# A hybrid decoder block on one core: block sums begun earlier in the attention, nine modulation rows moved into the values' and gates' products

## Chip, core and metric

The kernel runs on one core of one Trainium2 chip. The metric is the device time of one execution in microseconds; the median of several executions is given. All data are f32. Activations are kept transposed: features on the 128 partitions, the 512 tokens along the free axis.

The engines are named as in the profile: PE is TensorE (PEld its weight loads), DVE is VectorE, ACT is ScalarE, POOL is GpSimd, SP is SyncE, which issues most of the DMAs. Each engine works through its own queue in the order in which the program gave it the instructions.

## The reference, cut to what matters

```python
mod = silu(c) @ w_ada + b_ada                  # 9 vectors of 1024: shift, scale, gate of three sub-layers
u = rmsnorm(h) * (1 + sc1) + sh1
h = h + 0.5 * gt1 * swiglu(u)                  # first feed-forward
u = rmsnorm(h) * (1 + sc2) + sh2
h = h + gt2 * token_mixing(u)                  # <- the change is here
u = rmsnorm(h) * (1 + sc3) + sh3
h = h + 0.5 * gt3 * swiglu(u)                  # second feed-forward
return rmsnorm(h)

def token_mixing(u):                           # u: 512 x 1024
    p, q, k, v, gate_logits = split(u @ w_in)  # 256, 768, 768, 768, 2048 columns
    y_pool = multiscale_pool(p)                # trailing means over 2, 4, 8, 16 tokens
    q, k = rope(q), rope(k)                    # 12 heads of 64
    # three groups of four heads, dilations 1, 4, 16, causal windows;
    # the groups are merged by their softmax denominators
    y_attn = merged_dilated_attention(q, k, v)
    g_pool, g_attn = split(sigmoid(gate_logits))
    return (g_pool * (y_pool @ w_pb) + g_attn * (y_attn @ w_ab)) @ w_out
```

## The kernel before

**Matmuls in three parts.** Each f32 operand is split into a high part (ACT copies it into a rounded format: `whi`, `UH`) and a low part (DVE subtracts: `wlo`, `UL`), and each product is three matmuls: high x high, high x low, low x high. So each weight tile costs one DMA, one copy of 128 x 1024 on ACT (line 378) and one subtraction of the same size on DVE (line 390).

**Products in 2 x 2 blocks.** Wide products (values, gates, feed-forward) are computed in seven half-size block products in place of eight, in the manner of Strassen. These need sums of blocks of the weights (DVE, line 313, and DMAs that accumulate, issued by POOL, line 321) and sums of blocks of u. For the token mixer `mix_sums` makes the sums of u: `whole(i)` adds high and low part of a quarter of u (line 1323), `x0`, `x1`, `x2`, `x3` subtract such quarters from each other (lines 1334 and 1335), `hi(i)` and `lo(i)` split the results (ACT line 1327, DVE line 1331), and `last` writes the fourth one back into `UH` and `UL`. All are of 128 x 1024. The sums stand in buffers `x0`, `x1`, `x2` and `q0`; the split parts go to `uc`, `s0`, `k0`, `x2`, `v1`, `x0`.

**Modulation rows.** The 72 rows of `w_ada` (128 outputs each) are worked off in the background: `bg` makes DVE multiply one row of 128 x 1024 by silu(c) and add it up (line 449, in `ada_do`), then `bg_fetch` queues the DMA of a next row on SP (line 441) into a buffer of the list `ada_free`, as far ahead as `ada_depth` allows. A DMA into a buffer that is still being read waits, and SP's queue behind it waits too. `ada_stop` bounds how far the rows go.

**Order in `mix`.** The order is written out by hand. After the head (queries and keys of group 0) and the values of group 0 come two pool tiles, then eight tiles of queries and keys of groups 1 and 2 (`mm_tile`, 24 matmuls of 128 x 512 each), and then

- `value_duo`: the values of groups 1 and 2, in seven block products P0 to P6 of 24 matmuls of 128 x 256, on three PSUM banks A, B, C. The list of products is A (P0), B, A, C, A, B, A: each time that A is used again, a copy on ACT (line 1816) has carried away what it held. Bank C, into which A is copied after P0, is the bank of the last query and key tile.
- `gate_duo`, four times: seven block products each for the gates; the first in `mix`, the others in `merge_out`, which also does the branches and the output product.

`hooks` places other work at positions 0 to 7 inside a query and key tile (before the matmuls of that eighth): a list of pairs (position, function). At position 5 stand the attention's steps for group 0: values of the step before last, transposes (line 1486), scores (line 1453), exponentials (`at_exp`: reductions and maxima on DVE, lines 1469 and 1471, exponentials on ACT, line 1474). The rotary embedding of a tile is `rope_a` after it (ACT line 1394, DMAs on SP that exchange partitions, DVE multiply with the tile's bank, line 1398) and `rope_b` in the next tile at position 6 (DVE lines 1416 and 1420). The steps for groups 1 and 2 lie in the middle of P2, P4 and P6 of `value_duo` and of P1, P3 and P5 of the first `gate_duo` (the argument `within`); the argument `beside` holds what is done after a product.

Weights are fetched into three buffers and split three to four tiles ahead (`look`). The fetch of a tile is queued on SP when the program has given out the last use of a buffer.

The positions of the sums in the kernel before:

```python
sums = {4: [(7, lambda: u["whole"](0))],
        5: [(1, lambda: u["whole"](2)), (4, u["x0"]), (6, lambda: u["hi"](0)), (7, lambda: u["whole"](1))],
        6: [(1, u["x2"]), (3, u["x1"]), (5, lambda: u["lo"](0)), (7, lambda: u["whole"](3))],
        7: [(0, lambda: u["hi"](1)), (0, lambda: u["hi"](2)), (1, u["x3"]), (3, lambda: u["lo"](2)),
            (5, lambda: u["lo"](1))]}
```

Tiles 0 to 3 hold a modulation row each at position 7, tile 1 another at position 2: rows 51 to 55. Row 56 follows in the first gate block, rows 57 to 59 in the block after it.

Of the kernel before, what the change touches and what calls it, by code (L numbers as in the profile page):

```python
# [8 lines left out]
F32 = mybir.dt.float32  # L9
# [5 lines left out]
P = 128  # L15
T = 512
HT = 256
D = 1024
# [147 lines left out]
class Kernel:  # L166
# [5 lines left out]

    def plan(self):
        (i1, o1), mix, (i2, o2) = chunk_widths()
        self.chunks = []
        for name, ws in (("wf1i", i1), ("wf1o", o1), ("wmix", mix), ("wf2i", i2), ("wf2o", o2)):
# [267 lines left out]
    def ada_do(self, j, n=1):  # L444
        t, mod = self.adat.pop(j), self.mod[:, j:j + 1]
        for i in range(n):
            c = slice(i * D // n, (i + 1) * D // n)
            o = self.part if i else mod
            self.nc.vector.scalar_tensor_tensor(t[:, c], t[:, c], 1.0, self.cond[:, c], op0=OP.mult, op1=OP.mult,
                                                accum_out=o)  # L450
            if i:
                self.nc.vector.tensor_tensor(mod, mod, o, op=OP.add)
        if self.ada_free is not None:
            self.ada_free.append(t)

    def ada_fin(self, which, j0, j1, g=None):
# [273 lines left out]
    def step(self):  # L730

        self.now += 1
        due = [f for t, f in self.put if t <= self.now]
        self.put = [x for x in self.put if x[0] > self.now]
        for f in due:
            f()
# [874 lines left out]
    def mix(self):  # L1611
# [6 lines left out]
        mp = outer.enter_context(tc.tile_pool(name="mx", bufs=1))  # L1618

        x = [mp.tile([P, D], F32, name=f"x{i}") for i in range(3)]  # L1620
# [4 lines left out]
        with tc.tile_pool(name="rt", bufs=1) as self.rt, tc.tile_pool(name="aw", bufs=2) as self.aw:  # L1625
# [19 lines left out]
            self.bg_fetch()  # L1645
            self.head(1, bk, AF.Exp, [self.bg] * 5)
            assert self.ada_next == 45 and not self.adat, self.ada_next
            self.ada_free, self.ada_stop, self.ada_depth = list(x), 56, 2
            self.bg_fetch()

            to = [(self.qt[0], 0), (self.qt[0], 1), (self.kt[0], 0), (self.kt[0], 1)]
# [14 lines left out]
            for n in range(4):  # L1666
# [3 lines left out]
                b = self.nb()  # L1670
# [22 lines left out]
            def hooks(new, extra=(), between=()):  # L1693
                sc, old = pipe
                todo = [(self.at_values, old), (self.at_turn, sc), (lambda f: f(), between), (self.at_scores, new),
                        (self.at_exp, new)]
                h = {5: [lambda f=f, u=u: f(u) for f, us in todo for u in us]}
                for k, f in extra:
                    h.setdefault(k, []).append(f)
                pipe[0], pipe[1] = list(new), sc  # L1700
                return h


            todo = [x for n in range(4) for x in ([(0, n, hp) for hp in range(2)], [])]
            self.p1 = mp.tile([P, D], F32, name="s0")[:, :528]
            for t in range(2):
                self.pool_diff(t, self.mm_tile(hooks(todo.pop(0), [(7, self.bg)])))
            todo += [[], []]
            rest = []
            u = self.mix_sums([*x, self.qt[0]], [[wide(mp, "uc"), wide(mp, "s0")], [wide(ma, "k0"), wide(mp, "x2")],  # L1710
                                                 [wide(ma, "v1"), wide(mp, "x0")]])
            sums = {4: [(7, lambda: u["whole"](0))],
                    5: [(1, lambda: u["whole"](2)), (4, u["x0"]), (6, lambda: u["hi"](0)), (7, lambda: u["whole"](1))],
                    6: [(1, u["x2"]), (3, u["x1"]), (5, lambda: u["lo"](0)), (7, lambda: u["whole"](3))],
                    7: [(0, lambda: u["hi"](1)), (0, lambda: u["hi"](2)), (1, u["x3"]), (3, lambda: u["lo"](2)),
                        (5, lambda: u["lo"](1))]}
            for n, (dst, hp) in enumerate((y[g], hp) for g in (1, 2) for y in (self.qt, self.kt) for hp in range(2)):
                more = [(2, self.bg)] if n == 1 else []
                if n == 6:
                    self.X, self.retired = [self.AR, self.cs, self.v23.rearrange("p c f -> p (c f)")[:, D:]], []  # L1720
                    self.ready = True
                b = self.mm_tile(hooks(todo.pop(0), rest + more + sums.get(n, [(7, self.bg)])))
                rt = [self.scratch(2 * i + hp)[:, :T] for i in range(2)]
                self.rope_a(b, dst, hp, *rt)

                rest = [(6, lambda dst=dst, hp=hp, w=rt[1]: self.rope_b(dst, hp, w))]


            assert self.ada_next == 56 and not self.adat, self.ada_next

            def clear():
                v.memset(self.fT.bitcast(F32), 0.0)
# [3 lines left out]
            g23 = [[(1, c, hp) for hp in range(2)] for c in range(4)]  # L1736
            step = lambda c=None: [lambda: [f() for f in hooks(g23[c] if c is not None else [])[5]]]
            p5 = self.ev[:, 2 * T:3 * T]
            self.value_duo(p5, {0: rest[0][1], 1: u["last"]}, {2: step(0), 4: step(1), 6: step(2)})

            def rows():
                self.ada_free, self.ada_stop, self.ada_depth = [self.qt[2]], 60, 1
                self.bg_fetch()

            def third():
# [3 lines left out]
                self.pool_map(two(ma, "k2"), two(mp, "x1"))  # L1749

            used = self.gate_duo(self.qt[1], self.kt[1], p5, lambda n=1: None,
                                 {2: lambda: (self.at_swap(), rows()), 3: clear, 4: self.at_merge, 5: self.bg, 6: third}, {},
                                 {1: step(3), 3: step(), 5: step()})
            at = [t[:, i * T:(i + 1) * T] for i in range(2) for t in (self.qt[1], self.kt[1])]
            spread = [self.bS[1], self.bO] + self.bT
# [6 lines left out]
        def second():  # L1762
            self.at_high(0)
            self.at_y(spread, 1)

        self.merge_out(at, {0: lambda: (self.at_fT(spread[0]), self.bg()), 1: ends, 2: second, 3: lambda: (self.at_high(1), self.at_low(0)),
                            4: lambda: self.at_low(1), 5: self.bg, 6: self.bg}, ma, mp)
        outer.close()

# [189 lines left out]
    def build(self):  # L1959
        nc, tc, ctx, a = self.nc, self.tc, self.ctx, self.a  # L1960
        ctx.enter_context(tc.manual_schedule())
        per = ctx.enter_context(tc.tile_pool(name="per", bufs=1))
        psum = ctx.enter_context(tc.tile_pool(name="psum", bufs=1, space=bass.MemoryType.PSUM))
        self.plan()
        tl = lambda n, w, dt=F32: per.tile([P, w], dt, name=n)
        self.free = [tl(f"raw{i}", CW) for i in range(3)]

        self.hi, self.lo = tl("whi", RING, F32R), tl("wlo", RING, F32R)
        self.vecs = tl("vecs", 106)
        self.Hall = tl("H", KT * T)  # L1970
        self.H = [self.Hall[:, k * T:(k + 1) * T] for k in range(KT)]
        tl("pad0", 16)
        self.UHv = tl("UH", KT * T, F32R)
        cst, self.eps = tl("cst", 163), tl("eps", 1)
        tl("pad1", 16)
        self.ULv = tl("UL", KT * T, F32R)
        self.UH, self.UL = ([x[:, k * T:(k + 1) * T] for k in range(KT)] for x in (self.UHv, self.ULv))
        self.AR = tl("AR", 2 * T)
        self.acc, self.R = self.AR[:, :T], self.AR[:, T:]
        self.mod, self.part = tl("mod", 72), tl("part", 1)  # L1980
        self.hpi, self.r4 = tl("hpi", 1), tl("r4", 4)
        early = ExitStack()
        ep = early.enter_context(tc.tile_pool(name="early", bufs=1))
        el = lambda n, w, dt=F32: ep.tile([P, w], dt, name=n)
        self.cond = el("cond", D)
        self.ones = tl("ones", P)
        self.invf, self.sign, self.icnt, self.ident = cst[:, 0:1], cst[:, 1:2], cst[:, 3:35], cst[:, 35:163]
        self.cst = cst
        self.cs = el("cs", 2 * T)
        self.cos, self.sin = self.cs[:, :T], self.cs[:, T:]  # L1990
        tl("pad", 32)
        self.ev, self.turn = tl("ev", 4 * T), 0
        self.tr = el("tr", 5 * P)
        self.pi = self.tr[:, 4 * P:].bitcast(I32)
        self.B = [psum.tile([P, T], F32, name=f"bank{i}") for i in range(8)]
        self.banks, self.bi = self.B[:6], 0
        self.adat = {}
        self.todo = []
        dram = ctx.enter_context(tc.tile_pool(name="dram", bufs=1, space=bass.MemoryType.DRAM))
        self.scr = dram.tile([T, 8], F32, name="scr")  # L2000
        self.scr2 = dram.tile([32, 2 * T], F32, name="scr2")

        self.ada_free, self.ada_depth = None, 3
        with self.open_ffn():
            self.ada_pool = ExitStack()
            self.adaw = self.ada_pool.enter_context(tc.tile_pool(name="f1a", bufs=4))
            self.put, self.now = [], 0
            self.startup()
            self.ffn(0, FIRST)
            self.sums.close()  # L2010
        self.mix()
        early.close()
        with self.open_ffn(True) as self.f2:
            self.sums, self.retired = self.open_sums(), []
            self.ffn2()
# [185 lines left out]
```

## Time and profile before

| | |
|---|---|
| median of 3 runs | 978.46 us (976.54 to 983.93) |
| profiled execution | 980.78 us, span of its instructions 977.9 us |
| mean granted clock of PE | 0.993 |
| PE busy | 960.6 us (98%) |
| DVE busy | 850.9 us (87%) |
| ACT busy | 549.4 us (56%) |
| POOL busy | 90.8 us (9%) |
| moved by DMA | 173.67 MB |

Times in the views are microseconds from the first instruction of the span. In a timeline each row has the start, the duration, the engine, the line, the operation, what it writes and reads, and in brackets how long the engine was idle before it and what ended this. In the windows each row has the stretch, its length, the busy time of PE, PEld, DVE, ACT and POOL with the number of instructions, the clock that PE was granted as a share of full speed, the share of the DMA engines that was busy, and GB/s.

### The profile page before, as it was taken

How to read it: one execution, taken by the hardware profiler on the slowest of the kernel's cores; microseconds unless marked ns; L12 is line 12 of the kernel's file. 1: busy time of each engine (PE TensorE's matmuls, PEld its weight loads, DVE VectorE, ACT ScalarE, POOL GpSimd, SP SyncE). 2: the span in 40 equal slices, each digit the busy share in tenths (PEclk: the TensorE clock that was granted, in tenths of full speed). 3: DMA queues.
4: the chain of work that ended last, by engine and by line, in shares of the span. 5: the costliest groups of instructions: out<-in, count | busy, mean ns of one | idle time of the engine just before them, and what ended most of it. 6: DMA issues, size and time to landing. Idle time of an engine off the chain costs nothing.

```text
span 977.9 us, 18361 instructions
## 1 busy us (share of the span) xinstructions
PE 960.6 (98%) x7366; PEld 905.3 (93%) x7366; DVE 850.9 (87%) x1255; ACT 549.4 (56%) x837; POOL 90.8 (9%) x107
## 2 busy tenths in 40 slices
PE   9999999999999999998999999999999999999997
PEld 7888999999999899777898998898999999999997
DVE  7989999899998788899668887989899888989885
ACT  5443666565745553554675553465666657566655
POOL 0000100110100003810000000000101010110002
PEclk9999999999999999998999999999999999999999
DMA  9856785776868458634447655722766766665632
GB/s 350 280 181 249 208 235 148 208 198 152 235 178 251 138 170 272 215 103 115 112 132 222 166 130 174 252 93 89 194 150 195 173 151 164 171 172 142 169 80 87
DMA packets 54088, 173.67 MB, mean 178 GB/s; under 512 B 7793, under 2 KB 10481, under 8 KB 54002
## 3 DMA queue, kind: packets, MB, share of 16 engines
q1 hardware_dynamic: 44272, 140.24, 43.3%
q0 software_dynamic: 9152, 31.72, 18.0%
q8 instruction: 57, 0.93, 0.4%
q10 hardware_dynamic: 578, 0.53, 0.2%
q14 instruction: 29, 0.24, 0.1%
HBM read 135.36 MB, written 2.24 MB: 141 GB/s over the span
## 4 chain that ended last, share of the span: by engine, by line
PE 84%; DVE 9%; issue 2%; ACT 2%; DMA 2%; POOL 0%; SPq 0%; POOLq 0%; DVEq 0%; ACTq 0%
PE bank L752 12%; PE bank L753 12%; PE bank L754 12%; PE bank L422 8%; PE bank L423 8%; PE bank L424 8%; PE bank L1112 4%; PE bank L1113 4%; PE bank L1111 4%; DVE wlo L390 2%; PE bank L2123 2%; PE bank L2127 1%; PE bank L2125 1%; DMA cs<-wada 1%; ACT prob L1474 1%
## 5 line engine op out<-in xcount | busy, mean ns | idle before, releaser
L390 DVE TENSOR_TENSOR wlo<-raw,whi 128x1024 fp32r<-128x1024 f32 (+3 forms) x155 | 167.5, 1092 | 36.5 <-ACT whi L378 36.3
L752 PE MATMUL bank<-UH,whi 128*128 128x256 f32 x672 | 186.1, 277 | 0.0
L753 PE MATMUL bank<-UL,whi 128*128 128x256 f32 x672 | 185.7, 276 | 0.0
L754 PE MATMUL bank<-UH,wlo 128*128 128x256 f32 x672 | 185.7, 276 | 0.0
L390 DVE TENSOR_TENSOR wlo<-X,whi 128x1024 fp32r<-128x1024 f32 (+3 forms) x138 | 142.7, 1047 | 16.9 <-ACT whi L378 16.7
L378 ACT ACTIVATE whi<-raw 128x1024 fp32r<-128x1024 f32 (+3 forms) x155 | 142.9, 939 | 20.7 <-DMA raw<-wf1o 8.7
L378 ACT ACTIVATE whi<-X 128x1024 fp32r<-128x1024 f32 (+3 forms) x138 | 123.5, 918 | 51.1 <-DVE X L313 46.8
L752 PEld LDWEIGHTS bank<-UH,whi 128*128 128x128 f32 x672 | 126.3, 188 | 2.1 <-issue 1.9
L753 PEld LDWEIGHTS bank<-UL,whi 128*128 128x128 f32 x672 | 126.2, 188 | 0.0
L754 PEld LDWEIGHTS bank<-UH,wlo 128*128 128x128 f32 x672 | 126.2, 188 | 0.0
L754 PE MATMUL bank<-SH,wlo 128*128 128x256 f32 x408 | 112.7, 276 | 0.2 <-DVE wlo L390 0.2
L752 PE MATMUL bank<-SH,whi 128*128 128x256 f32 x408 | 112.7, 276 | 0.0
L753 PE MATMUL bank<-SL,whi 128*128 128x256 f32 x408 | 112.6, 276 | 0.0
L422 PE MATMUL bank<-UH,whi 128*128 128x512 f32 (+1 forms) x272 | 92.7, 341 | 0.0
L423 PE MATMUL bank<-UL,whi 128*128 128x512 f32 (+1 forms) x272 | 91.8, 337 | 0.1
L424 PE MATMUL bank<-UH,wlo 128*128 128x512 f32 (+1 forms) x272 | 91.5, 336 | 0.0
L754 PEld LDWEIGHTS bank<-SH,wlo 128*128 128x128 f32 x408 | 76.6, 188 | 0.4 <-DVE wlo L390 0.4
L752 PEld LDWEIGHTS bank<-SH,whi 128*128 128x128 f32 x408 | 76.6, 188 | 0.0
L753 PEld LDWEIGHTS bank<-SL,whi 128*128 128x128 f32 x408 | 76.6, 188 | 0.0
L1111 PE MATMUL bank<-HI,whi 128*128 128x256 f32 x224 | 61.8, 276 | 0.0
L1112 PE MATMUL bank<-HK,whi 128*128 128x256 f32 x224 | 61.8, 276 | 0.0
L1113 PE MATMUL bank<-HI,wlo 128*128 128x256 f32 x224 | 61.8, 276 | 0.0
(430 smaller groups left out, 2462.7 us busy)
## 6 DMA issues: line engine op xcount, KB each, us to landing
raw<-wmix SPq DMA_DIRECT2D x44, 512.0 KB, 4.4
raw<-wf1i SPq DMA_DIRECT2D x32, 512.0 KB, 5.7
raw<-wf2i SPq DMA_DIRECT2D x30, 512.0 KB, 3.7
ada<-wada SPq DMA_DIRECT2D x23, 512.0 KB, 5.6
X<-raw POOLq DMA_DIRECT2D x23, 512.0 KB, 5.3
x<-wada SPq DMA_DIRECT2D x22, 512.0 KB, 5.0
X<-wf2i SPq DMA_DIRECT2D x14, 512.0 KB, 4.6
X<-wf1i SPq DMA_DIRECT2D x11, 512.0 KB, 4.6
```

The lines of the kernel that those rows point to most:

```text
L378: self.nc.scalar.activation(self.hi[:, y], r[:, x], AF.Copy)
L390: self.nc.vector.tensor_tensor(self.lo[:, y], r[:, x], self.hi[:, y], op=OP.subtract)
L422: M(ps, hi, uh, start=start, stop=False)
L423: M(ps, hi, ul, start=False, stop=False)
L424: M(ps, lo, uh, start=False, stop=stop)
L752: M(o, hi, uh, start=start and p == 0 and k == 0, stop=False, skip_group_check=True)
L753: M(o, hi, ul, start=False, stop=False, skip_group_check=True)
L754: M(o, lo, uh, start=False, stop=k == 3, skip_group_check=True)
L1111: M(o, hi, uh, start=start and m % 2 == 0 and k == 0, stop=False, skip_group_check=True)
L1112: M(o, hi, ul, start=False, stop=False, skip_group_check=True)
L1113: M(o, lo, uh, start=False, stop=k == 1, skip_group_check=True)
L2123: M(b, hi, self.UH[k], start=k == 0, stop=False)
```

## The change

The sums of u start at tile 1 in place of tile 4, and are spread over tiles 1 to 7. The modulation rows stop at 51 in place of 56 before the value block: the five in tiles 0 to 3 are taken out. Rows 51 to 59 are then placed after P1, P3 and P5 of `value_duo`, after products 0, 2, 5 and 6 of the first gate block and, as before, after products 5 and 6 of the next one. They use the buffer `x1`, loaded one row at a time, and from row 57 on `q2`; `x1` is not given back after its last row (`ada_gone`), since `pool_map` needs its place.

```diff
-        if self.ada_free is not None:
+        if self.ada_free is not None and t is not self.ada_gone:
             self.ada_free.append(t)
...
-            self.ada_free, self.ada_stop, self.ada_depth = list(x), 56, 2
+            self.ada_free, self.ada_stop, self.ada_depth = list(x), 51, 2
...
-            sums = {4: [(7, lambda: u["whole"](0))],
-                    5: [(1, lambda: u["whole"](2)), (4, u["x0"]), (6, lambda: u["hi"](0)), (7, lambda: u["whole"](1))],
-                    6: [(1, u["x2"]), (3, u["x1"]), (5, lambda: u["lo"](0)), (7, lambda: u["whole"](3))],
-                    7: [(0, lambda: u["hi"](1)), (0, lambda: u["hi"](2)), (1, u["x3"]), (3, lambda: u["lo"](2)),
-                        (5, lambda: u["lo"](1))]}
+            sums = {1: [(1, lambda: u["whole"](0))], 2: [(1, lambda: u["whole"](2)), (5, u["x0"])],
+                    3: [(0, lambda: u["hi"](0)), (1, lambda: u["whole"](1))], 4: [(1, u["x2"]), (4, u["x1"])],
+                    5: [(1, lambda: u["whole"](3)), (3, lambda: u["hi"](1)), (4, u["x3"]), (6, lambda: u["lo"](0))],
+                    6: [], 7: [(0, lambda: u["hi"](2)), (1, lambda: u["lo"](2)), (4, lambda: u["lo"](1))]}
...
-                more = [(2, self.bg)] if n == 1 else []
...
-                b = self.mm_tile(hooks(todo.pop(0), rest + more + sums.get(n, [(7, self.bg)])))
+                b = self.mm_tile(hooks(todo.pop(0), rest + sums.get(n, [])))
...
-            assert self.ada_next == 56 and not self.adat, self.ada_next
+            assert self.ada_next == 51 and not self.adat, self.ada_next
+            row = mp.tile([P, D], F32, name="x1")
+            self.ada_free, self.ada_stop, self.ada_depth = [row], 60, 1
+            self.bg_fetch()
...
-            self.value_duo(p5, {0: rest[0][1], 1: u["last"]}, {2: step(0), 4: step(1), 6: step(2)})
+            self.value_duo(p5, {0: rest[0][1], 1: lambda: (u["last"](), self.bg()), 3: self.bg, 5: self.bg}, {2: step(0), 4: step(1), 6: step(2)})
...
             def rows():
-                self.ada_free, self.ada_stop, self.ada_depth = [self.qt[2]], 60, 1
+                self.ada_free.append(self.qt[2])
+                self.ada_gone = row
                 self.bg_fetch()
...
-                                 {2: lambda: (self.at_swap(), rows()), 3: clear, 4: self.at_merge, 5: self.bg, 6: third}, {},
+                                 {0: self.bg, 2: lambda: (self.at_swap(), self.bg(), rows()), 3: clear, 4: self.at_merge, 5: self.bg, 6: lambda: (third(), self.bg())}, {},
...
-        self.merge_out(at, {0: lambda: (self.at_fT(spread[0]), self.bg()), 1: ends, 2: second, 3: lambda: (self.at_high(1), self.at_low(0)),
+        self.merge_out(at, {0: lambda: self.at_fT(spread[0]), 1: ends, 2: second, 3: lambda: (self.at_high(1), self.at_low(0)),
```

More of the change, by code (lines that the diff above doesn't have):

```diff
@@ L2001, in build @@
         self.scr2 = dram.tile([32, 2 * T], F32, name="scr2")
-        self.ada_free, self.ada_depth = None, 3
+        self.ada_free, self.ada_depth, self.ada_gone = None, 3, None
         with self.open_ffn():
```

## The prediction

> **What bounds the kernel now.** I read the page first, then the waits of TensorE (PE), then the stretch of the change in 2 us windows, then the timelines of PE, VectorE (DVE) and ScalarE (ACT) there.
>
> ```profile
> span 977.9 us, 18361 instructions
> ...
> PE 960.6 (98%) x7366; PEld 905.3 (93%) x7366; DVE 850.9 (87%) x1255; ACT 549.4 (56%) x837; POOL 90.8 (9%) x107
> ```
>
> PE is busy 98% of the span, and the change leaves its matmuls as they are. So all that can be won is PE idle time and time at a lowered clock. The view of PE's waits between 380 and 620 us, which holds the whole token mixer, has two rows (total, times, longest):
>
> ```profile
> PE bank L1834 <- ACT bank L1816: 4.3, 1, 4.3
> PE bank L1834 <- ACT v L1816: 2.3, 1, 2.3
> ```
>
> Both are in `value_duo`. The windows show what follows each wait (columns: PE, weight loads, DVE, ACT, POOL busy, granted clock, DMA share, GB/s):
>
> ```profile
> 456.00:458.00 2.00, 0.00 (x0) 0.00 (x0) 1.97 (x3) 0.00 (x0) 0.00 (x0) 1.00 1.03 197
> 458.00:460.00 2.00, 0.25 (x1) 0.25 (x2) 2.00 (x3) 0.88 (x2) 0.00 (x0) 0.66 0.01 0
> 460.00:462.00 2.00, 2.00 (x10) 2.00 (x11) 1.46 (x3) 2.00 (x4) 0.00 (x0) 0.50 0.00 0
> 462.00:464.00 2.00, 2.00 (x16) 1.78 (x16) 1.97 (x3) 1.04 (x2) 0.00 (x0) 0.50 0.53 127
> 464.00:466.00 2.00, 2.00 (x16) 1.78 (x13) 2.00 (x5) 0.00 (x0) 0.00 (x0) 0.63 0.62 193
> ...
> 478.00:480.00 2.00, 0.58 (x2) 0.58 (x3) 0.00 (x0) 2.00 (x6) 0.00 (x0) 0.78 0.36 102
> 480.00:482.00 2.00, 2.00 (x11) 2.00 (x10) 1.66 (x2) 1.26 (x2) 0.00 (x0) 0.50 0.00 0
> 482.00:484.00 2.00, 2.00 (x23) 1.60 (x23) 2.00 (x4) 0.00 (x0) 0.87 (x1) 0.86 0.36 70
> ```
>
> After the wait that ends at 459.75, PE runs at clock 0.50 until about 465.5 (the 0.63 window is half-rate for three quarters): 5.7 us at half rate, 2.9 us lost. After the one that ends at 479.42 it is half-rate until about 482.55 (0.86): 3.1 us, 1.6 lost. **At stake: 4.3 + 2.9 + 2.3 + 1.6 = 11.1 us.**
>
> Next, why PE waits. I call the value block's products P0 to P6, and tiles 0 to 7 the query and key tiles of groups 1 and 2.
>
> ```profile
> 449.61 0.28 PE L1834 MATMUL bank<-whi,UH 128*128 128x256 f32 x1
> 452.43 0.38 PE L1834 MATMUL bank<-whi,uc 128*128 128x256 f32 x1
> 459.75 0.58 PE L1834 MATMUL bank<-whi,k 128*128 128x256 f32 x1 [4.32 <-ACT bank L1816]
> 470.58 1.04 PE L1486 MATMUL bank<-cst,prob 128*128 128x128 f32 x8
> 471.56 1.16 PE L1453 MATMUL bank<-k,q 64*128 64x128 f32 x16
> 479.42 0.58 PE L1834 MATMUL bank<-whi,UH 128*128 128x256 f32 x1 [2.26 <-ACT v L1816]
> ```
>
> ```profile
> 459.12 0.58 ACT L1816 ACTIVATE bank<-bank 128x512 f32<-128x512 f32 x1 [5.83 <-DVE k L1398]
> ...
> 468.43 0.58 ACT L1816 ACTIVATE v<-bank 128x512 f32<-128x512 f32 x1
> ...
> 478.79 0.57 ACT L1816 ACTIVATE v<-bank 128x512 f32<-128x512 f32 x1
> ```
>
> P0 starts at 449.61, P1 at 452.43: 2.8 us a product. P2 (459.75) waits until ACT has copied bank A into bank C at 459.12, and ACT waited 5.83 us for DVE, whose rope multiply (L1398) of tile 7 still had to read bank C, 9 us after PE had filled it. P6 (479.42) waits for the copy of 478.79, which stands in ACT's queue behind the exponentials of an attention step, and these behind DVE's reductions. Both are a late DVE:
>
> ```profile
> 402.48 1.22 DVE L449 SCALAR_TENSOR_TENSOR x<-x,cond 128x1024 f32<-128x1024 f32 x1
> ...
> 404.47 0.69 DVE L1398 TENSOR_TENSOR q<-bank,cs 128x512 f32<-128x512 f32 x1 [0.77 <-ACT tr L1394]
> ...
> 407.48 2.08 DVE L449 SCALAR_TENSOR_TENSOR x<-x,cond 128x1024 f32<-128x1024 f32 x1
> ...
> 412.64 1.61 DVE L449 SCALAR_TENSOR_TENSOR x<-x,cond 128x1024 f32<-128x1024 f32 x1
> ...
> 421.03 1.22 DVE L449 SCALAR_TENSOR_TENSOR x<-x,cond 128x1024 f32<-128x1024 f32 x1
> ...
> 425.51 0.69 DVE L1416 TENSOR_TENSOR rt<-rt,cs 128x512 f32<-128x512 f32 x1 [1.52 <-DMA rt<-tr]
> ...
> 426.84 1.22 DVE L449 SCALAR_TENSOR_TENSOR x<-x,cond 128x1024 f32<-128x1024 f32 x1
> ...
> 433.45 1.22 DVE L1323 TENSOR_TENSOR x<-UH,UL 128x1024 f32<-128x1024 f32 x1
> ...
> 458.34 0.68 DVE L1398 TENSOR_TENSOR k<-bank,cs 128x512 f32<-128x512 f32 x1
> ...
> 461.84 0.68 DVE L1416 TENSOR_TENSOR rt<-rt,cs 128x512 f32<-128x512 f32 x1
> ...
> 465.44 0.41 DVE L1469 CUSTOM_DVE_ANT_0 prob<-bank,masks 128x256 f32<-128x256 f32 x1
> ...
> 469.99 1.23 DVE L390 TENSOR_TENSOR wlo<-v,whi 128x1024 fp32r<-128x1024 f32 x1 [2.70 <-ACT whi L378]
> ...
> 475.75 0.42 DVE L1469 CUSTOM_DVE_ANT_0 prob<-bank,masks 128x256 f32<-128x256 f32 x1
> ```
>
> ```profile
> 450.00:460.00 10.00, 5.68 (x48) 5.45 (x47) 9.93 (x12) 2.49 (x4) 0.89 (x1) 0.93 0.51 124
> 460.00:470.00 10.00, 10.00 (x71) 9.55 (x72) 6.66 (x17) 6.59 (x15) 0.00 (x0) 0.73 0.49 159
> ...
> 490.00:500.00 10.00, 10.00 (x100) 9.39 (x99) 4.48 (x13) 7.28 (x16) 0.00 (x0) 1.00 0.37 109
> ```
>
> DVE works 9.93 of the 10 us before 460. From 426 to 460 it has one queue without a hole. So here DVE is the bound: PE follows it at three points, tile 7's multiply (458.34), the first attention step's reductions (465.44), the second's (475.75).
>
> **The change, part by part.** *Five modulation rows (51 to 55) leave tiles 0 to 3.* They are the five L449 rows above. A 1.22 us operation holds the queue 1.14 us (426.84 to the accumulator read at 427.99). The one at 402.48 is worth nothing: the multiply at 404.47 then waits for ACT anyway. The others give 2.0 + 1.5 + 1.1 + 1.1, and 0.2 for the bias addition after the last: 6.0 us.
>
> *Four of the sums (whole 0, whole 2, x0, whole 1) move from tiles 4 to 6 into tiles 1 to 3.* Their number is the same. But two run while GpSimd still computes the pools; there the row at 407.48 took 2.08 where its like takes 1.22. Whether a sum does too isn't shown; between 1.14 and 2.0 each I take 2.0 and 1.9, since a row of the same size in the same place took that: 1.6 us lost, at least 0. The 1.5 us hole ahead of 425.51 is filled by the sums: 1.5 won. A new hole of some 1.0 us opens in tile 5: x2 and x1 now stand ahead of tile 4's reductions, so ACT gets to its next weight copy 1 us later. Sum: -6.0 + 1.6 - 1.5 + 1.0 = **-4.9, so tile 7's multiply starts at 453.4 (bounds 452 to 455)**. ACT's copy then ends at 454.1; P2 wants it at 449.6 + 2 x 2.8 = 455.2. The first wait goes, and its half clock with it.
>
> *What is late next.* Between the multiply (458.34) and the first step's reductions (465.44) DVE needs 7.1 us: two weight remainders, the rope sum at 461.84, a third remainder, the last sum. Row 51 now stands there as well: 1.1. So the reductions start at 453.4 + 7.1 + 1.1 = 461.6. From them to the end of ACT's copy, 468.43 + 0.58 - 465.44 = 3.6 us: 465.2. P4 needs this copy. PE reaches P4 at 455.2 + two products (5.6) + 1.1 for the step's scores + 0.5, since the last scores read the rope sum, done at 453.4 + 3.5 + 1.3 = 458.2 where they could have ended at 457.7: 462.4. **A new wait of about 2.8 us ahead of P4.** In the old run this copy ended at 469.0.
>
> *P6.* From the first reductions to the second, 475.75 - 465.44 = 10.3 us, of them 2.70 idle for ACT (469.99), which stays. Row 52 adds 1.1: 461.6 + 11.4 = 473.0. Copy done 3.6 later: **P6 starts at 476.6 in place of 479.42, 2.8 us earlier.** PE is free for it at 465.2 + 4.9 (P4 with 2.1 of transposes and scores) + 2.8 = 472.9, or 1.7 later if the clock halves after P4's wait; either is before 476.6, so that halving costs nothing, and a second wait of 2 to 3.7 us is left.
>
> *Loads.* A row's load is queued on SP behind the release of the single buffer `x1`, so it stops the weight loads behind it until DVE has done the row before.
>
> ```profile
> raw<-wmix SPq DMA_DIRECT2D x10, 512.0 KB, 5.0
> ```
>
> Row 52's load waits for row 51 (done 461.5), ahead of the second load of the gate block, which would have been free about 459. Landed 5.0 us later, that is 467, just when DVE gets to the sum that reads it. Cost taken 0.3, bounds 0 to 3.
>
> *Rows 53 to 59.* They lie in the gate block and the first block after it, where DVE is busy 4.48 of 10 us and PE waits nowhere. I take 0; the cover is DVE's idle time. The row after 56 goes into another buffer (`q2`), so SP doesn't wait there. One row less in the merge: 0.
>
> *Clock after P6.* The old wait of 2.26 us cost 1.6; one of 2 to 3.7 us costs between 0 and 2.9. I take the same 1.6.
>
> **Sum: -2.8 + 0.3 = -2.5 us** on the profiled execution of 980.78 (span 977.9, 2.9 around it), so 978.3. The median of the runs is 978.46, 2.3 lower; from there **976.0 us**.
>
> **Rivals.** (a) *Both waits go.* If DVE reaches the first step 3 us earlier than I think (the sums at 1.14 under GpSimd, no new hole: 2.6 us), P4 doesn't wait, and the second wait shrinks too: down to -11.1, 967.4; half of it, 971. For it: every wait is the same late DVE. Against: two of the five rows come back ahead of the last wait. (b) *No halving after P6*, as a short wait split over two stretches of the clock's watch might pass: -4.1, 974.4. For it: the new wait needn't lie as the old one did. Against: clock 0.50 after 2.26 us. [...] (c) *Nothing moves*: ACT and not DVE sets P4 and P6; DVE idled 2.70 us for it before 469.99. Then 978 to 979. (d) *Slower: the row on SP starves the gate weights.* Place: row 52 ahead of the second gate load. Price: DVE waits for that load in front of the second step's reductions, one us of PE for each us. It decides from 2.8 us on, so if three loads of 512 KB queued at once take over 8 us where one takes 5.0; at 10 us, P6 at 481.5 with its half clock, +2 to +3: 981. Against it: DMA share 0.5 there. (e) *The change doesn't do what it says*, a row's load or a buffer's release holding the sums back to their old places: as (c).
>
> **How the numbers follow.** Forecast (-1 to -4 us) 0.55; (a) 0.17, of it 0.07 by nearly all; (b) 0.08; (c) and (e) 0.12; (d) 0.08. Leaving out the end of (a) and half of (d): 968.5 to 981. The runs of before spread from 976.54 to 983.93, so about 1% (9.8 us) is what a measurement can tell from no change: faster 0.07 (the end of (a)), slower 0.02 (from (d)), within 0.91.
>
> **What would show it.** Right: no PE wait for the copy from bank A to bank C; tile 7's multiply about 4 us after PE's last matmul in its bank, not 9; a wait of 2 to 3 us on L1834 ahead of P4 for a copy into v23, and one ahead of P6; the clock at 0.5 in one or two windows; no wait in the gates. Wrong: DVE with holes before tile 7 (then its relief was smaller), no wait at P4 (rival a), DVE waiting for a DMA ahead of a weight sum (rival d), or a new PE wait after 500 us.

## The result, and the profile after

The changed kernel takes 976.81 us in the median of 20 runs (974.04 to 978.88), the kernel before 979.38 (976.54 to 983.93). The ratio is 0.9973, 95% interval 0.9962 to 0.9984: **2.6 us less, 0.3%**. The profiled execution has a span of 975.8 us where before had 977.9. Lines of the changed kernel lie two further down from `value_duo` on (L1834 is L1836, L1816 is L1818), and those of the experiments up to six.

The head of the page, with instructions as before and nearly the same busy times:

```profile
span 975.8 us, 18361 instructions
...
PE 957.7 (98%) x7366; PEld 902.1 (92%) x7366; DVE 849.4 (87%) x1255; ACT 548.7 (56%) x837; POOL 90.7 (9%) x107
```

PE's waits between 380 and 620 us (total, times, longest):

```profile
PE bank L1836 <- ACT v L1818: 5.6, 2, 3.5
PE bank L1544 <- DVE x L1609: 0.8, 1, 0.8
PE bank L1504 <- DVE v L1850: 0.8, 1, 0.8
PE bank L1486 <- ACT prob L1474: 0.3, 1, 0.3
```

Before there were two, of 4.3 and 2.3 us. The one for the copy from bank A into bank C is gone. Two for copies into `v23` are there, together 5.6 us, and three short ones that are new. PE's timeline says where (start, duration, operation, idle time before it):

```profile
449.93 0.28 PE L1836 MATMUL bank<-whi,UH 128*128 128x256 f32 x1
...
452.76 0.28 PE L1836 MATMUL bank<-whi,uc 128*128 128x256 f32 x1
...
455.58 0.28 PE L1836 MATMUL bank<-whi,k 128*128 128x256 f32 x1
...
464.79 0.39 PE L1836 MATMUL bank<-whi,v 128*128 128x256 f32 x1 [2.10 <-ACT v L1818]
...
476.30 0.39 PE L1836 MATMUL bank<-whi,UH 128*128 128x256 f32 x1 [3.45 <-ACT v L1818]
```

P0, P1 and P2 follow each other 2.83 us apart, without a hole. P4 waits 2.10 us and P6 3.45. So 6.6 us of waiting became 7.5 in other places. The waiting itself didn't shrink; in this profile the gain is the half clock that followed both waits of before (4.5 us by the prediction's reckoning) and follows neither of these. The windows behind the two waits:

```profile
464.00:466.00 2.00, 1.21 (x10) 1.21 (x11) 0.28 (x1) 2.00 (x5) 0.00 (x0) 1.00 0.94 365
...
478.00:480.00 2.00, 1.21 (x17) 0.80 (x18) 2.00 (x4) 0.14 (x1) 0.87 (x1) 1.00 0.00 0
```

The granted clock is 1.00 throughout, where the same stretch of before has 0.50. This isn't how most runs went: 16 of the 20 were granted 0.996 or 0.997 in the mean, against 0.999 here. Yet those 16 average 976.5 us and the two at 0.999 976.3, so the difference hardly shows in the time. A stretch of 3.41 us at half clock takes 0.0017 off the mean (1.7 of 975.8 us), so in most runs there is room for one such stretch; where it lay there isn't known.

DVE's timeline, with the rows that answer to those of before (L390 makes the low part of a weight tile, the weight remainder):

```profile
406.28 1.23 DVE L390 TENSOR_TENSOR wlo<-raw,whi 128x1024 fp32r<-128x1024 f32 x1 [0.27 <-ACT whi L378]
407.42 2.08 DVE L1323 TENSOR_TENSOR x<-UH,UL 128x1024 f32<-128x1024 f32 x1
...
413.20 1.21 DVE L390 TENSOR_TENSOR wlo<-raw,whi 128x1024 fp32r<-128x1024 f32 x1
414.33 1.24 DVE L1323 TENSOR_TENSOR x<-UH,UL 128x1024 f32<-128x1024 f32 x1
...
451.73 0.68 DVE L1398 TENSOR_TENSOR k<-bank,cs 128x512 f32<-128x512 f32 x1
452.78 1.23 DVE L390 TENSOR_TENSOR wlo<-raw,whi 128x1024 fp32r<-128x1024 f32 x1 [0.37 <-ACT whi L378]
454.53 1.23 DVE L390 TENSOR_TENSOR wlo<-raw,whi 128x1024 fp32r<-128x1024 f32 x1 [0.53 <-ACT whi L378]
456.29 0.69 DVE L1416 TENSOR_TENSOR rt<-rt,cs 128x512 f32<-128x512 f32 x1 [0.53 <-DMA rt<-rt]
...
461.17 0.42 DVE L1469 CUSTOM_DVE_ANT_0 prob<-bank,masks 128x256 f32<-128x256 f32 x1
...
466.87 1.22 DVE L313 TENSOR_TENSOR AR<-raw,raw 128x1024 f32<-128x1024 f32 x1
...
472.62 0.42 DVE L1469 CUSTOM_DVE_ANT_0 prob<-bank,masks 128x256 f32<-128x256 f32 x1
...
477.23 1.23 DVE L390 TENSOR_TENSOR wlo<-cs,whi 128x1024 fp32r<-128x1024 f32 x1 [2.75 <-ACT whi L378]
478.37 0.68 DVE L1850 TENSOR_TENSOR v<-v,bank 128x512 f32<-128x512 f32 x1
```

And ACT's:

```profile
464.16 0.58 ACT L1818 ACTIVATE v<-bank 128x512 f32<-128x512 f32 x1
...
475.67 0.57 ACT L1818 ACTIVATE v<-bank 128x512 f32<-128x512 f32 x1
476.15 1.05 ACT L378 ACTIVATE whi<-cs 128x1024 fp32r<-128x1024 f32 x1
```

Tile 7's multiply comes 6.6 us earlier than before (458.34 to 451.73). Of this 4.3 are left at the first step's reductions (465.44 to 461.17), 3.1 at the second's (475.75 to 472.62), and 3.1 at P6 (479.42 to 476.30).

### The profile page after: what moved, and what is told of

It is laid out like the page before. It is cut to its first block, busy times and chain, and to the rows that moved or that the text cites. A ratio compares the mean times of both kernels' runs of the same rounds, so it can differ in the third digit from the quotient of the medians.

```text
span 975.8 us, 18361 instructions
## 1 busy us (share of the span) xinstructions
PE 957.7 (98%) x7366; PEld 902.1 (92%) x7366; DVE 849.4 (87%) x1255; ACT 548.7 (56%) x837; POOL 90.7 (9%) x107
## 4 chain that ended last, share of the span: by engine, by line
PE 74%; DVE 12%; DMA 5%; issue 4%; ACT 3%; SPq 1%; POOL 0%; ACTq 0%; POOLq 0%; DVEq 0%
PE bank L752 12%; PE bank L754 12%; PE bank L753 12%; PE bank L423 6%; PE bank L424 6%; PE bank L422 6%; PE bank L1113 4%; PE bank L1111 4%; PE bank L1112 4%; DVE wlo L390 3%; DMA x<-wada 2%; PE bank L2125 2%; PE bank L2127 1%; PE bank L2129 1%; ACT prob L1474 1%
## 5 line engine op out<-in xcount | busy, mean ns | idle before, releaser
L390 DVE TENSOR_TENSOR wlo<-raw,whi 128x1024 fp32r<-128x1024 f32 (+3 forms) x155 | 166.2, 1084 | 34.5 <-ACT whi L378 34.2
L390 DVE TENSOR_TENSOR wlo<-X,whi 128x1024 fp32r<-128x1024 f32 (+3 forms) x138 | 143.1, 1050 | 17.3 <-ACT whi L378 17.2
```

The costliest lines, as they stand in the source:

```text
L390: self.nc.vector.tensor_tensor(self.lo[:, y], r[:, x], self.hi[:, y], op=OP.subtract)
```

## The experiments

**The theory (A)** is the prediction's: DVE's queue sets the attention steps' reductions, these the exponentials on ACT, these the copies behind them in ACT's queue, and these P4 and P6; a microsecond on DVE is about one of PE there. Its rivals: the rows are harmless where they stand, and ACT's own order or the clock decides; or the rows cost as much in the gates as in the value block. Points in the table are counted from the start of P0 in the same profile, since P0 itself starts between 447.3 and 452.6 us in them. L1544 is the first matmul that turns the merge's factors, 65 us after P0; L510, 185 us after it, one that makes the column sums of squares in the output product. Waits are PE's from 380 to 660 us. All ratios differ from 1 by less than 1%; the intervals in brackets tell each from 1 but that of e1.

| kernel | ratio to before | P4 | P6 | L1544 | L510 |
|---|---|---|---|---|---|
| before | 1 | 19.62 | 29.81 | 68.43 | 187.74 |
| changed | 0.9973 [0.9962, 0.9984] | 14.86 | 26.37 | 65.50 | 185.23 |
| e1, no rows in the value block | 1.0002 [0.9989, 1.0014] | 13.31 | 23.68 | 66.69 | 188.52 |
| e2, sums in the old places | 1.0022 [1.0011, 1.0033] | 19.41 | 30.92 | 69.27 | 188.48 |
| e3, five more operations early | 1.0022 [1.0011, 1.0033] | 16.44 | 27.95 | 66.20 | 186.20 |
| e4, copies ahead of exponentials | 0.9985 [0.9974, 0.9997] | 12.71 | 20.52 | 66.60 | 185.82 |
| e5, rows spread | 0.9956 [0.9940, 0.9973] | 14.17 | 24.52 | 64.19 | 185.39 |
| e6, e5 with a new order | 0.9924 [0.9906, 0.9942] | 12.44 | 21.50 | 59.23 | 181.00 |
| e7, changed with the new order | 0.9930 [0.9913, 0.9947] | 12.44 | 21.50 | 63.24 | 184.07 |
| e8, changed, once more | 0.9972 [0.9958, 0.9987] | 14.87 | 26.37 | 64.67 | 184.03 |
| e9, e6 with the ninth row in the gates | 0.9922 [0.9909, 0.9934] | 12.47 | 21.53 | 58.72 | 179.57 |
| e10, e6 with the ninth row in the merge | 0.9912 [0.9897, 0.9927] | 12.44 | 21.50 | 59.14 | 178.58 |

**e1: the two rows ahead of P4 and P6 (and the third) moved into the gates.**

```diff
-self.value_duo(p5, {0: rest[0][1], 1: lambda: (u["last"](), self.bg()), 3: self.bg, 5: self.bg}, ...
+self.value_duo(p5, {0: rest[0][1], 1: u["last"]}, ...
...
-{0: self.bg, 2: ..., 3: clear, 4: self.at_merge, 5: self.bg, ...
+{0: self.bg, 1: self.bg, 2: ..., 3: clear, 4: lambda: (self.at_merge(), self.bg()), 5: self.bg, ...
...
+ merge_out, position 0: a row behind at_fT
```

> The changed kernel with rows 51 to 53 taken out of the value block: rows 51 to 56 lie after products 0, 1, 2, 4, 5 and 6 of the first gate block, 57 to 59 in the block after it. Theory A (VectorE's queue sets P4 and P6, one us for one us): two rows of 1.14 us less ahead of the second step's reductions, so P6 starts 2.3 us earlier against P0 than in the changed kernel, the wait ahead of P4 falls from 2.1 to about 1 and the one ahead of P6 from 3.5 to about 2.3; the time is 2.3 us (1.5 to 3) below the changed kernel, ratio to before about 0.995. Theory B (ScalarE's queue sets P4 and P6, the rows lie in its shadow): both waits stay, ratio 0.997. Theory C (the gates have no room for the rows): P6 earlier as in A, but new PE waits of 1 to 3 us in the gate blocks, ratio 0.997 or above.

P6 comes 2.69 us earlier than in the changed kernel, as (A) has it for two rows of some 1.15 us and less waiting. But all of it is lost, and 3.3 us more by L510. The waits and DVE's row behind them:

```profile
PE bank L1544 <- DVE x L1609: 4.0, 1, 4.0
PE bank L1836 <- ACT v L1818: 3.0, 2, 2.3
```

```profile
503.91 1.23 DVE L313 TENSOR_TENSOR cs<-raw,AR 128x1024 f32<-128x1024 f32 x1 [3.49 <-DMA raw<-wmix]
```

DVE stands 3.49 us for a weight load; two more rows follow ahead of L1609; PE waits 4.0 us for it and then runs at half clock from 513.77 to 520.59. So the gates have no room for three rows, as the expectation's theory C had it, though DVE is idle more than half of the ten microseconds that the prediction quoted for them. How much of this is the load and how much the rows is not shown: the load is queued on SP behind that of a row, but SP had stood before that until 496.94 for the DMA of the attention's statistics, and DVE waits for the same load without the move too, 1.95 us in the kernel before and 2.40 in the changed one:

```profile
507.29 1.22 DVE L313 TENSOR_TENSOR cs<-raw,AR 128x1024 f32<-128x1024 f32 x1 [1.95 <-DMA raw<-wmix]
```

```profile
505.62 1.23 DVE L313 TENSOR_TENSOR cs<-raw,AR 128x1024 f32<-128x1024 f32 x1 [2.40 <-DMA raw<-wmix]
```

**e2: the rows as changed, the sums in their old places.**

```diff
-sums = {1: [(1, lambda: u["whole"](0))], 2: ...
+sums = {4: [(7, lambda: u["whole"](0))], 5: ...   (as before)
```

> The changed kernel's rows (51 to 59 in the value and gate blocks), with the block sums back at their old positions in tiles 4 to 7. Theory A (the sums must move for the rows' room to be of use): VectorE stands idle in tiles 1 to 3 and is as late as before from tile 4 on; PE waits again for the copy from bank A to C ahead of P2, 3.5 to 4.3 us, and P6 comes 1.5 to 2.5 us later than before because of rows 51 and 52; ratio to before 1.001 to 1.004. Theory B (taking the rows out is what helps, wherever the sums stand): no wait ahead of P2, ratio 0.997.

```profile
PE bank L1837 <- ACT v L1819: 3.6, 2, 1.8
PE bank L1837 <- ACT bank L1819: 3.1, 1, 3.1
```

The wait for the copy from A into C is back with 3.1 us: taking five rows out does little if the sums stay late. P6 is 1.1 us later than before: P2 won 1.2 us (8.96 after P0 in place of 10.15), and rows 51 and 52 now stand on DVE ahead of P6 with some 1.15 each. So the rows' move is of no use without the sums'.

**e3: the changed kernel with five multiply-and-accumulate operations of a row's size and no DMA, in tiles 0 to 3.** They work on a buffer that nobody reads then.

```diff
+extra = {0: [(7, dummy)], 1: [(2, dummy), (7, dummy)], 2: [(7, dummy)], 3: [(7, dummy)]}
-b = self.mm_tile(hooks(todo.pop(0), rest + sums.get(n, [])))
+b = self.mm_tile(hooks(todo.pop(0), rest + sums.get(n, []) + extra.get(n, [])))
```

> The changed kernel with five more VectorE operations of 128x1024 (a product with an accumulator, as a modulation row, on a buffer that nothing reads, no DMA) where the five rows stood in tiles 0 to 3. Theory A (the load of VectorE is what counts): of 6 us some 1.5 fall into idle time, so tile 7's multiply starts 4 to 4.5 us later than in the changed kernel, PE waits about 1 us ahead of P2, and P6 starts 2 to 3 us later; ratio to before 0.999 to 1.001. Theory B (the order of the sums is what counts): as the changed kernel, 0.997.

```profile
PE bank L1840 <- ACT v L1822: 4.0, 2, 2.1
PE bank L1486 <- ACT prob L1474: 1.6, 1, 1.6
PE bank L1453 <- DVE k L1420: 1.1, 1, 1.1
```

Tile 7's multiply starts at 456.91, 5.2 us later than in the changed kernel; P0 itself starts 2.7 later. The wait of 1.6 lies ahead of P0, at transposes of a tile, the one of 1.1 at scores in P2; against P0, P4 and P6 are 1.6 later. The wait ahead of P2, expected at about 1 us, is 0.2. Five operations without a DMA take back more than the gain, which is more than I had expected: DVE's time decides here, and no load is needed for it. So the sums' move is of no use while DVE has that much to do ahead of P0.

**e4: in the value block the exponentials go behind the copy of the product on ACT, ahead of the weight copies that follow.**

```diff
-{2: step(0), 4: step(1), 6: step(2)})
+{2: part(0), 4: part(1), 6: part(2)}, {2: exps(0), 4: exps(1), 6: exps(2)})
...
+            if i in then:            # in value_duo, after the copy of product i
+                then[i]()
```

> The changed kernel with the reductions and exponentials of the value block's three attention steps queued after the copy of the product that they follow, not ahead of it. Theory A (P4 and P6 wait for VectorE's late queue only through ScalarE's order; behind it the next late thing is the same queue): the waits for the copies ahead of P4 and P6 go (2.1 and 3.5 us), but the transposes in the middle of P4 then wait about 1 us for the exponentials, and the value products of the step in the middle of P6 wait for VectorE's subtraction into v23 until about 1 us before they ran in the changed kernel; 1 us (0 to 2) below the changed kernel, ratio 0.996. Theory B (ScalarE's order alone is the bound): 4 to 5.5 us below, ratio 0.992.

```profile
PE bank L1504 <- DVE v L1852: 5.7, 1, 5.7
```

P4 and P6 don't wait any more, and P6 starts 5.85 us earlier. But in the middle of P6 PE waits 5.7 us for DVE's subtraction into `v23`, and the clock is then 0.5 from 476.24 to 483.07. Its chain: the subtraction (477.55) stands on DVE behind a weight remainder (476.41), this waits 2.21 us for a weight copy (`whi<-cs`) on ACT (475.34), and that stands behind the exponentials (from 473.36). The expectation had named this wait, as the next point of the same chain, but reckoned with 1 us less time in all (ratio 0.996); 0.9985 came, which can't be told from the changed kernel's 0.9973. The halved clock behind the wait wasn't in it.

**e5: row 51 back in tile 0, none in the value block, one more in the output product.**

```diff
-self.ada_free, self.ada_stop, self.ada_depth = list(x), 51, 2
+self.ada_free, self.ada_stop, self.ada_depth = list(x), 52, 2
...
-b = self.mm_tile(hooks(todo.pop(0), rest + sums.get(n, [])))
+b = self.mm_tile(hooks(todo.pop(0), rest + sums.get(n, [(7, self.bg)])))
...
+ value_duo without rows; merge_out, position 0: a row behind at_fT
...
-for _ in range((2, 2, 3, 2, 1)[m]):
+for _ in range((2, 3, 3, 2, 1)[m]):
```

> The changed kernel, with its gate block left alone (rows after products 0, 2, 5, 6), but no row in the value block: row 51 goes back to the end of tile 0, where VectorE stood idle for 2 us, one row to product 0 of the block after the gates, one to the output product. Theory A (VectorE's queue sets P4 and P6): as in the run with all rows in the gates, P6 comes 2.3 to 3 us earlier against P0 than in the changed kernel; and since the gates keep four rows, no wait of 4 us follows there; 1.5 to 3 us below the changed kernel, ratio to before 0.994 to 0.996. Theory B (whatever PE wins in the value block is given back in the gates, because their chain of weight loads behind the statistics' DMAs sets PE there): a PE wait of 2 us or more at the factors' transposes (L1544) and 0.997.

P6 is 1.85 us earlier, less than the 2.3 to 3 expected, and the gates have no new wait (0.9 at L1544). The ratio is below the changed kernel's by 0.0017, with intervals that overlap; at L510 the row in the output product costs 1.8 us.

**e6: e5, and in the value block the exponentials behind the copy and behind the weight copies, the subtraction ahead of the next weights.**

```diff
-{0: rest[0][1], 1: u["last"]}, {2: step(0), 4: step(1), 6: step(2)})
+{0: rest[0][1], 1: u["last"], 2: exps(0), 4: exps(1), 6: exps(2)}, {2: part(0), 4: part(1), 6: part(2)})
...
-self.look(3 if i in (0, 2) else 4)
+self.look(3 if i in (0, 2, 5) else 4)
...
-            if i in (0, 2):
+            if i in (0, 2, 5):
```

> As the kernel with the rows spread, and in the value block the reductions and exponentials of an attention step are queued behind the copy of the product and behind the weight copies of the next tile, and the subtraction into v23 ahead of the next weights. Theory A (what remains is the order of the queues): no wait for a copy ahead of P4 and P6, a wait of 1 us or less at the transposes of P4, about none for v23; P6 starts 5 to 6 us earlier than in the changed kernel, no halved clock; 4 to 6 us below the changed kernel, ratio 0.991 to 0.993. Theory B (given back in the gates): the value block ends as early, PE waits 2 to 4 us at L1544, ratio 0.994 to 0.996.

**e7: the changed kernel with this order alone.**

> The changed kernel with the order of the queues of the run before alone, its rows left where they are. Theory A (rows 51 to 53 and the order each cost their own): between the changed kernel and the run with both, P6 3 to 4 us earlier than in the changed kernel, ratio 0.993 to 0.995. Theory B (the rows hold VectorE so far behind that the order is of no use, as when the copy alone was put first): the wait moves to the transposes and the value products, ratio 0.997 or above.

e6 has no wait in the value block but 0.7 us in all at transposes. What it has left from 380 us on, above 1 us, is one row:

```profile
PE bank L510 <- DVE AR L624: 2.4, 1, 2.4
```

e7 has these:

```profile
PE bank L1544 <- DVE x L1609: 2.6, 1, 2.6
PE bank L1504 <- DVE v L1852: 1.7, 1, 1.7
```

Added to the changed kernel, the order is worth at least as much as the change itself: P6 at 21.50 in both, 4.9 us earlier than in the changed kernel, and 0.9930. What it would give to the kernel before wasn't tried. The rows' places decide how much of it is left at L1544 (63.24 against 59.23), but e6 pays 2.4 us for its row in the output product, and the times of e6 and e7 can't be told apart.

**e8: the changed kernel once more beside e5 to e7.**

> The changed kernel once more, beside the three others. All theories: ratio to before 0.997, with waits of about 2 and 3.5 us ahead of P4 and P6; whether the clock is halved after them may differ from the first profile, since neither fills a whole stretch of 3.4 us.

0.9972 where the first comparison gave 0.9973; P4 and P6 agree within 0.01 us, and the mean clock of the profile is 0.999 again. L1544 and L510 come 0.8 and 1.2 us earlier than in the first profile, and PE doesn't wait at L1544: further from P0, differences of about a microsecond between two rows of the table say nothing.

**e9 and e10: e6 with that row elsewhere**, in the second gate block or between the merge's branches and the first output product.

```diff
-for _ in range((2, 3, 3, 2, 1)[m]):
+for _ in range((2, 2, 3, 2, 1)[m]):
...
+ e9: merge_out, position 4: a row behind at_low(1)
+ e10: one more self.bg() ahead of the first output products
```

> Rows 51 in tile 0, none in the value block, exponentials behind the copies (as in the run before with both), but the ninth row stands after product 4 of the second gate block in place of the output product. The run with both was at 0.9924 and kept one PE wait of 2.4 us at L510 for that row. If the wait is bought off by moving the row: that wait gone, no new one, 1.5 to 2.4 us less, ratio 0.990 to 0.991. If the gate blocks have no room for it either: a wait for a weight remainder or a transposes' operand of 1 to 4 us in the gates, ratio 0.992 or above.

> The same with the ninth row between the merge's branches and the first output products, ahead of the first output sums. If DVE has idle time there: the wait of 2.4 us at L510 gone, ratio 0.990 to 0.991. If DVE is late for the first output products: a wait at the output products for the parts of the merge, about 1.2 us, ratio 0.9915 to 0.993.

The wait at L510 is gone in both. e9 has one of 1.3 us in the second gate block in its place, and its time is that of e6 (0.9922 and 0.9924), as the expectation had it for gates without room:

```profile
PE bank L752 <- ACT gc L1777: 1.3, 1, 1.3
```

In e10 no wait of PE from 380 to 660 us is longer than 0.4.

e10, at 971.0 us against 979.58, has **the lowest ratio: 0.9912 [0.9897, 0.9927]**. In its profile L510 comes 2.4 us earlier than in e6. Its interval overlaps with those of e6 and e9, so that it beats these is not shown by times alone; that it beats the changed kernel is.

## Why the prediction was right, step by step

**What bounds: right, with ACT's order as it stood.** e3 makes DVE late by 5.2 us and loses the gain; e1 takes two operations off DVE and P6 comes 2.69 us earlier. But e7 leaves the rows where they are and P6 comes 4.87 us earlier by another order on ACT and DVE: the lateness and the order make the wait together.

**Tile 7's multiply: right in kind, 1.7 us mis-sized.** Predicted 453.4, with 452 to 455 as bounds; it came at 451.73, just outside them. I had priced both sums beside GpSimd at about a row's 2 us. The one at 407.42 took 2.08, the other (414.33) 1.24, which is 0.7 of the 1.7. More came from what I had left out: the other operations beside GpSimd change too. Two weight remainders took about 2 us in the kernel before,

```profile
405.42 2.14 DVE L390 TENSOR_TENSOR wlo<-raw,whi 128x1024 fp32r<-128x1024 f32 x1 [0.26 <-ACT whi L378]
...
414.79 1.99 DVE L390 TENSOR_TENSOR wlo<-raw,whi 128x1024 fp32r<-128x1024 f32 x1
```

and take 1.23 and 1.21 (406.28 and 413.20). With two smaller operations, one shorter and one longer by about 1 us, this is worth 1.6 us. DVE's holes came to 0.3 less than reckoned, and DVE reached the first of the tiles' multiplies 0.85 later than in the profile before (405.32 for 404.47). The 454.1 given for the end of ACT's copy is its start; the end would have been 454.7, still ahead of P2.

**First reductions: right by two errors that cancel.** Predicted 461.6, measured 461.17. The 7.1 us from multiply to reductions were taken from before, where DVE waited once, 0.54 us for a weight copy. Reaching the stretch earlier, it waited three times: 0.37 and 0.53 for weight copies and 0.53 for the DMA of the rotary exchange, whose sum starts at 456.29 where I had 456.9. What is late next had three answers, and I had named only DVE's own work.

**P4's wait: right.** 2.10 us against 2.8: the copy ended at 464.74 in place of 465.2, and PE was there at 462.69 in place of 462.4.

**P6: right.** 476.30 against 476.6; its wait of 3.45 us lies within the 2 to 3.7.

**SP: 0.3 predicted, nothing found.** DVE reaches the sum at 466.87 and has no idle time before it. SP's queue shows the row's load and the two weight loads behind it without a delay between them:

```profile
461.28 0.33 SPq L441 DMA_DIRECT2D x<-wada  x1
461.70 0.86 SPq L296 DMA_DIRECT2D raw<-wmix  x2
```

Rival (d) is out at the place that it names. Further on, in the gates, DVE does wait for a weight load queued behind a row's, 2.40 us; but it waited 1.95 there in the kernel before and waits 1.57 in e8, so that no cost of the change is shown there either.

**Rows in the gates: 0 predicted; short.** A wait of 0.8 at L1544 is new in this profile, though not there in e8's, and another of 0.8, in both profiles, lies in the middle of P6, at L1504: the `v23` subtraction starts on DVE at 478.37, behind a remainder that waited 2.75 us for ACT's `whi<-cs`, itself behind the exponentials (476.15). I had followed the chain only as far as P6's start. The windows of the gates could not tell either: that DVE is idle for 5.5 of 10 us says nothing of whether a row stands in front of the one operation that PE needs next.

**Clock after P6: 1.6 predicted, 0 in this profile.** Rival (b)'s condition came true there: the clock stayed at 1.00 after a wait of 3.45 us. With no halving the sum would have been -4.1; the two unforeseen waits (0.8 each) took as much back. That a short wait split over two stretches of the clock may pass was (b)'s assumption; what the profiles show of it stands in the last section. In the profile: -3.1 at P6, about -4.4 within P6 for the half clock not paid, -3.6 after L1504's wait, -2.6 at L1544, -2.2 at L510, -2.1 at the end. So the forecast of -2.5 met -2.1 in the profile and -2.57 between the medians partly by terms that cancelled; in the runs with a lower mean clock the half clock may have been paid as forecast. The forecast time of 976.0 lies 0.8 below the measured one, as it started from the median of three runs, 978.46, where twenty give 979.38. Rival (a) failed for the reason given only in part: with the two rows out of the way (e1), waits of 3.0 us for the copies into `v23` are left of 5.6. e6 and e7 show that the order on ACT, which I had taken as fixed, was where the rest lay. (The 971 given in (a) for half of 11.1 us should be 972.9; nothing follows from it.)

## What to carry to other kernels

Relief of a bound engine reaches only the next point where the chain crosses another queue: follow the chain past the wait you remove to the two waits after it, and ask for each whether it comes from lateness or from the order in a queue. Here the order took the changed kernel from 0.9972 to 0.9930, at least as much as shifting work had given. With only the copy that PE waits for put ahead of the exponentials (e4), the wait moved on into P6; in e7 the weight copies and the subtraction went ahead as well, and which of these two counts wasn't tried. Background work is best put where the queue behind it holds nothing that is due; an engine's busy share over ten microseconds doesn't tell: in the gates of the kernel before DVE was busy for 4.48 of 10 us, and in e1, with three rows moved there, PE waits 4.0 us.

## What the runs showed of the hardware

**In these profiles the half clock goes by stretches of 3.41 us.** In the clock records every lowered stretch around this place lasts 3.41 or 6.83 us, and within a run their starts lie on one grid of 3.413 us: in before they are 458.65, 479.13 and, at the end of the kernel, 974.07, which is 6 and 145 times 3.413 apart; in e1 472.81 and 513.77, 12 times. The windows below lie on the grid. PE's busy time in the grid stretch just ahead of a drop (the windows' first column after the length), in before, e1, e5, e7 and e2:

```profile
455.24:458.65 3.41, 0.19 (x2) 0.00 (x0) 3.34 (x5) 0.00 (x0) 0.00 (x0) 1.00 0.81 154
...
475.72:479.13 3.41, 1.44 (x13) 1.23 (x11) 1.81 (x11) 2.32 (x9) 0.00 (x0) 1.00 0.88 226
```

```profile
469.39:472.81 3.42, 1.11 (x10) 0.91 (x9) 0.74 (x5) 3.42 (x10) 0.00 (x0) 1.00 0.55 145
...
510.35:513.77 3.42, 0.69 (x6) 0.48 (x5) 3.39 (x7) 2.09 (x4) 0.88 (x1) 1.00 0.51 96
```

```profile
470.47:473.88 3.41, 1.26 (x12) 1.07 (x10) 1.78 (x11) 2.35 (x9) 0.00 (x0) 1.00 0.86 216
```

```profile
508.74:512.15 3.41, 1.15 (x9) 0.81 (x10) 3.41 (x5) 2.32 (x4) 0.00 (x0) 1.00 0.67 126
```

```profile
466.08:469.50 3.42, 1.62 (x14) 1.42 (x14) 1.02 (x6) 3.21 (x10) 0.00 (x0) 1.00 0.94 310
```

And the two in the changed kernel that share the longest wait, followed by no drop:

```profile
471.23:474.65 3.42, 1.62 (x14) 1.41 (x12) 3.18 (x13) 0.96 (x4) 0.00 (x0) 1.00 1.01 235
474.65:478.06 3.41, 1.76 (x16) 1.64 (x16) 0.83 (x1) 3.41 (x9) 0.00 (x0) 1.00 0.40 154
```

After a stretch at full clock in which PE was busy for 0.19 to 1.44 us of 3.41 (at most 42%) the clock is halved in the next; after 1.76 (52%) it isn't; after 1.62 (47%) it was halved in e2 and not in the changed kernel. So in these rows the share of a stretch that PE is busy goes with the drop, with the turn somewhere between 42 and 52%. A wait of 2.26 us that fell for 2.0 us into one stretch (before) was punished, and one of 3.45 that fell across two (1.80 and 1.65 us) was not. The length of a wait alone doesn't tell whether a drop follows. Counted from the start of the span, the first point of the grid lies at 1.3 us in before, 0.2 in the changed kernel and 1.8 in e1. Whether it also changes from run to run of one kernel wasn't tried; the mean clocks of 0.995 to 0.999 in the changed kernel's 20 runs would fit that.

**A DVE sum beside GpSimd took 2.08 or 1.24 us.** GpSimd's rows:

```profile
406.44 5.68 POOL L1584 TENSOR_TENSOR v<-v 128x525 f32<-128x525 f32 x3
...
414.56 2.16 POOL L1593 TENSOR_TENSOR ev<-ev,s 64x512 f32<-64x512 f32 x1
...
418.95 1.62 POOL L1593 TENSOR_TENSOR ev<-ev,s 64x512 f32<-64x512 f32 x1
```

The sum at 407.42 begins while GpSimd is in a chain of long operations, and takes 2.08. The one at 414.33 begins 0.2 us ahead of GpSimd's next long one; it takes 1.24, and GpSimd's 2.16 where the like takes 1.62, and 1.29 and 1.30 in the profile before. In both pairs the one that began later took longer than its like, 2.08 for 1.24 and 2.16 for 1.62 or less. No run here took GpSimd's part away, so that the overlap is the cause isn't shown.
